# A two-layer macaron transformer block on one Trainium2 core: pairing chunks 1 to 7 of the gated FFN in place of 0 to 5

## The chip, the cores and the metric

The kernel runs on one core of a Trainium2 chip, with no second core to wait for. The metric is device time in microseconds (us): the median of a few executions of the compiled program. Five engines matter here. PE (TensorE) multiplies matrices and accumulates in PSUM banks. DVE (VectorE) and ACT (ScalarE) prepare its operands and empty its banks. SP only issues the DMA transfers that bring weights from HBM, one after the other in a fixed order. POOL (GpSimd) has a few small operations. Each engine works through its own list in order and waits at semaphores for the others.

## The reference

The input is 256 tokens of width 1024, in fp32. Two layers each compute FFN 1, a token mixing of three mixers with one projection in and one out, and FFN 2, each with a residual and a LayerNorm. The part that the change touches is the gated FFN, with an inner width of 2816:

```python
def swiglu(x, w_gate, w_up, w_down):
    return (jax.nn.silu(x @ w_gate) * (x @ w_up)) @ w_down
...
x = layer_norm(ALPHA * x + 0.5 * swiglu(x, ffn1_gate[l], ffn1_up[l], ffn1_down[l]), ln1_g[l], ln1_b[l])
```

There are four such FFNs, named here by layer and place: (0,1), (0,2), (1,1) and (1,2). Between (0,1) and (0,2), and between (1,1) and (1,2), stands the mixing of that layer.

## The kernel before

**Arithmetic.** PE works on fp32 values that are split in two: `hi` is a rounded copy (ACT), `lo` the rest (DVE, `raw - hi`). Every product is three matmuls, hi·hi, hi·lo and lo·hi (`mm3`, L248 to L250, and `proj_chan`, L258 to L260). Weights stream from HBM in blocks of 128 x 1024 fp32 (512 KB) into five `raw` buffers, and from there by one cast and one subtraction (L190, L191) into twelve `hi` and twelve `lo` buffers. `ensure` issues the loads in the order of `_plan`, seven blocks ahead of the one that is being used. A `raw` buffer is free when its last reader is through.

**An FFN.** The inner width is cut into chunk 0 of 512 columns and chunks 1 to 9 of 256. For each chunk PE makes the gate product `pg`, ACT takes its Silu (`sg`, L421), PE makes the up product `pu`, and DVE multiplies the two (`h`, L426). Chunk 0 is made with tokens on the partitions (`tok`, twice 128 tokens), so its `h` has to be transposed by PE (`trans`, L439). Chunks 1 to 9 come out transposed (`chan`, 48 matmuls for each of `pg` and `pu`). `h` is then split into `hTh` and `hTl`, which are the stationary operands of the down projection.

**Pairs.** In three of the four FFNs (all but (0,1)) some chunks don't go through the down projection's eight block products but through seven, M1 to M7, by the Strassen-Winograd scheme. For that a pair of down blocks `ra`, `rb` is combined in `pair_operands`: `b11` and the cast of `rb` (operands 1, 2, 3), four subtractions in place in the `raw` buffers (L202), and then `rest`, which casts the sums `th`, `sh` (operands 5, 7 from `ra`, 4, 6 from `rb`). `rest` waits in the list `put_off` until some further blocks have been cast. The left operands need sums of `h` too (`left_sums`, L461 to L464). A chunk of 256 is one unit of seven products (21 matmuls with 512 columns); chunk 0 is two.

Before the change chunks 0 to 5 are paired. In iteration c (1 to 6) the order on PE is: `pg` of chunk c; M1, M2, M4, M5 of chunk c-1; `pu` of chunk c; M6, M7, M3 of chunk c-1. In these iterations `pg` and `pu` share one PSUM bank (`free`), since the other one (`held`) keeps M3. So `pu` can't start before `sg` has been read out of the bank, nor the next `pg` before `h` has. The four products in the middle stand between `pg` and `pu`, the three at the end between `pu` and the next `pg`. After iteration 6 `combine` adds M1 to M7 into the residual; chunks 6 to 9 go through plain products at the end (`down`).

**What sets the order.** The program is written as straight Python, and a scheduler turns it into a fixed list for each engine, by its own estimates of when data arrive. `high_priority` moves `sg` and `h` forward. Small loads hang behind a given transfer (`issue_after`): the LayerNorm's `lng` and `lnb` in iteration 2, seven small tensors of the mixing in iteration 4 of FFN 1.

Of the kernel before, what the change touches and what calls it, by code (L numbers as in the profile page):

```python
# [17 lines left out]
S = 256  # L18
# [15 lines left out]

def _paired(l, f):

    return 0 if (l, f) == (0, 1) else 6
# [26 lines left out]
def _plan():  # L64

    out = []
    for l in range(L):
        for f in (1, 2):
# [13 lines left out]
            for c, (f0, fw) in enumerate(CHUNKS):  # L82
                for name in ("g", "u"):
                    step = _step(l, f, name, c)
                    out += [((l, f, name, c), k, step * fw, True) for k in range(0, KC, step)]
                out += [((l, f, "d", c), k, 1024, True) for k in range(fw // 128)]
# [46 lines left out]
def _build(tc, A, out):  # L133
# [3 lines left out]
    with ExitStack() as es:  # L137
        pool = lambda name, bufs, **k: es.enter_context(tc.tile_pool(name=name, bufs=bufs, **k))
        cst = pool("cst", 1)
        rawp = pool("raw", 5)  # L140
        hip = pool("hi", 12)
        lop = pool("lo", 12)
# [24 lines left out]
        def ensure(i):  # L167
            while len(loaded) <= min(i, len(plan) - 1):
                key, k, n, split, o = plan[len(loaded)]
                src = A["ws"][o:o + 128 * n].rearrange("(p c) -> p c", p=128)  # L170
                if len(key) == 4 and key[2] == "d" and key[3] < _paired(*key[:2]):
# [21 lines left out]
                while put_off and put_off[0][0] < len(loaded) - 1:  # L193
                    put_off.pop(0)[1]()
# [195 lines left out]
        def ffn(l, f, lni, last=False, mid=None):  # L390
# [17 lines left out]
            def chan(name, c):  # L408

                w = kslices((l, f, name, c), 256)  # L410
                if c <= paired_chunks:
# [19 lines left out]
            def hpair():  # L431
                return (wk.tile([128, 512], F32R, name="hTh", tag="a"),
                        wk.tile([128, 512], F32R, name="hTl", tag="a"))

            def trans(h, t):
# [5 lines left out]
                if paired_chunks:  # L441
                    hf[t] = wk.tile([128, 4, 128], F32, name="hf", tag="w")
                    ACT.copy(hf[t].rearrange("p a b -> p (a b)"), tr)
                    tr = hf[t].rearrange("p a b -> p (a b)")
# [9 lines left out]
            hf = {}  # L454
# [3 lines left out]
            def left_sums(c, i, a11, a12, a21, a22):  # L458

                S = wk.tile([128, 4, 128], F32, name="S", tag="w")  # L460
                DVE.tensor_tensor(S[:, 0, :], a21, a22, ALU.add)  # L461
                DVE.tensor_tensor(S[:, 1, :], S[:, 0, :], a11, ALU.subtract)
                DVE.tensor_tensor(S[:, 2, :], a11, a21, ALU.subtract)
                DVE.tensor_tensor(S[:, 3, :], a12, S[:, 1, :], ALU.subtract)  # L464
# [3 lines left out]
                left[c, i] = {5: part(0), 6: part(1), 7: part(2), 3: part(3)}  # L468

            def left_side(c, i, m):  # L470
                if m in (3, 5, 6, 7):
                    return left[c, i][m]
                t, b = {1: (0, 0), 2: (0, 1), 4: (1, 1)}[m]
                return stationary(c, t, 2 * i + b)

            def paired(c, ms):

                for m in ms:
# [3 lines left out]
                    for i in range(CHUNKS[c][1] // 256):  # L482
                        w = blocks((l, f, "d", c))[2 * i]
                        mm3(M[m], left_side(c, i, m), w[m], c == 0 and i == 0,
                            c == paired_chunks - 1 and i == CHUNKS[c][1] // 256 - 1)
# [46 lines left out]
            else:  # L532
                for t in range(2):
# [3 lines left out]
                    h[t] = product(tok("u", t), sg)  # L537

            if paired_chunks:
                turns.append(1)  # L540
                free, held = f"gu{len(turns) % 2}", f"gu{1 - len(turns) % 2}"
            for c in range(1, n):
# [5 lines left out]
                if c <= paired_chunks:  # L548
                    if c == 1:
                        for i in range(2):  # L550
                            a = lambda t, b: hf[t][:, 2 * i + b, :]
                            left_sums(0, i, a(0, 0), a(0, 1), a(1, 0), a(1, 1))
                    paired(c - 1, (1, 2, 4, 5))
# [8 lines left out]
                if c <= paired_chunks:  # L562
                    paired(c - 1, (6, 7, 3))
                hT[c] = hpair()
                split_to(*hT[c], hc)
                if c < paired_chunks:
# [372 lines left out]
```

## Time and profile before

| what | value |
|---|---|
| runs | 998.08, 990.7, 993.01 us, median 993.01 |
| profiled execution | 994.34 us, its span 992.6 us |
| granted TensorE clock | 0.999 of full speed |
| PE busy | 969.1 us (98%), 6765 instructions |
| DVE busy | 734.8 us (74%) |
| ACT busy | 512.3 us (52%) |
| DMA | 183.19 MB, the weights' queue 55.0% of the 16 engines' span |
| FFN (0,2) | 312.12 to 498.46 us |
| FFN (1,1) | 498.46 to 685.25 us |
| FFN (1,2) | 799.32 to 984.65 us |

Times in the trace count from the span's start. A row of the timeline gives start, duration, engine, line, operation, output and inputs; in square brackets stands how long the engine had been idle before it, and what it waited for. Durations of neighbours overlap by some 0.05 to 0.17 us (an instruction's start, not its end, frees the place for the next), so a step is read from start to start.

### The profile page before, as it was taken

Reading aid. Unit: us, or ns where it says so; the run is one execution under the profiler, and the core shown is the slowest. Engines: PE = TensorE matmul, PEld = TensorE weight load, DVE = VectorE, ACT = ScalarE, POOL = GpSimd, SP = SyncE. Lnnn points to the kernel's source line nnn. Section 1 sums busy time; section 2 is a strip of 40 time slices with the busy share of each in tenths; the row PEclk is TensorE's granted clock in tenths of the full one; section 3 lists DMA queues with packets and bytes.
Section 4 is the critical chain, followed back from the end, with each engine's and each line's share of the span. In section 5 each row is a group of like instructions: output and inputs, shape, how many; then the busy total and the mean of one; then the engine's idle time right before and its main releaser. Section 6 shows DMA issues by size and latency. Waiting matters only on the chain.

```text
span 992.6 us, 16879 instructions
## 1 busy us (share of the span) xinstructions
PE 969.1 (98%) x6765; PEld 875.8 (88%) x6765; DVE 734.8 (74%) x1094; ACT 512.3 (52%) x730; POOL 19.8 (2%) x42
## 2 busy tenths in 40 slices
PE   7999999999999999999999999999999999999996
PEld 5899999899878799999879899998988778989995
DVE  5755454586869978877598888848678797888844
ACT  6644444256556655555255556534475555556520
POOL 1000000010000000000000000000000000000000
PEclk9999999999999999999999999999999999999999
DMA  7977566284323557677245667764742245757611
GB/s 256 344 237 226 181 194 193 96 324 147 111 86 128 179 180 236 194 253 233 86 151 171 233 214 253 237 200 148 256 149 80 84 158 170 253 196 232 213 60 43
DMA packets 53069, 183.19 MB, mean 185 GB/s; under 512 B 6656, under 2 KB 7168, under 8 KB 52992
## 3 DMA queue, kind: packets, MB, share of 16 engines
q1 hardware_dynamic: 52992, 182.12, 55.0%
q8 instruction: 53, 0.87, 0.4%
q14 instruction: 24, 0.20, 0.1%
HBM read 181.05 MB, written 1.05 MB: 183 GB/s over the span
## 4 chain that ended last, share of the span: by engine, by line
PE 74%; DVE 11%; DMA 9%; issue 3%; ACT 3%; SPq 0%; DVEq 0%; ACTq 0%
DMA raw<-in_ws 8%; PE pu L258 6%; PE pu L260 6%; PE pu L259 6%; PE pg L258 5%; PE pg L260 5%; PE pg L259 5%; PE y L248 4%; PE y L250 4%; PE y L249 4%; DVE raw L202 3%; PE pc L258 3%; PE pc L260 3%; PE pc L259 3%; DVE lo L263 3%
## 5 line engine op out<-in xcount | busy, mean ns | idle before, releaser
L191 DVE TENSOR_TENSOR lo<-raw,hi 128x1024 fp32r<-128x1024 f32 (+3 forms) x284 | 336.6, 1200 | 115.2 <-ACT hi L190 113.5
L190 ACT CAST hi<-raw 128x1024 fp32r<-128x1024 f32 (+3 forms) x284 | 289.8, 1034 | 247.4 <-PE pu L259 64.7
L258 PE MATMUL pu<-xTh,hi 128*128 128x256 f32 x576 | 161.7, 281 | 3.4 <-ACT sg L421 3.4
L258 PE MATMUL pg<-xTh,hi 128*128 128x256 f32 x576 | 161.6, 281 | 0.5 <-DVE h L426 0.5
L260 PE MATMUL pu<-xTh,lo 128*128 128x256 f32 x576 | 160.9, 279 | 0.0
L260 PE MATMUL pg<-xTh,lo 128*128 128x256 f32 x576 | 160.8, 279 | 0.0
L259 PE MATMUL pu<-xTl,hi 128*128 128x256 f32 x576 | 160.8, 279 | 0.0
L259 PE MATMUL pg<-xTl,hi 128*128 128x256 f32 x576 | 160.8, 279 | 0.0
L258 PEld LDWEIGHTS pu<-xTh,hi 128*128 128x128 f32 x576 | 108.0, 188 | 7.1 <-ACT sg L421 5.9
L263 ACT CAST hi<-raw 128x1024 fp32r<-128x1024 f32 x63 | 66.2, 1052 | 90.5 <-DVE raw L202 46.5
L258 PEld LDWEIGHTS pg<-xTh,hi 128*128 128x128 f32 x576 | 108.1, 188 | 2.3 <-DVE h L426 1.2
L259 PEld LDWEIGHTS pu<-xTl,hi 128*128 128x128 f32 x576 | 107.9, 187 | 1.2
L260 PEld LDWEIGHTS pu<-xTh,lo 128*128 128x128 f32 x576 | 108.2, 188 | 0.2
L259 PEld LDWEIGHTS pg<-xTl,hi 128*128 128x128 f32 x576 | 107.9, 187 | 0.5
L260 PEld LDWEIGHTS pg<-xTh,lo 128*128 128x128 f32 x576 | 108.2, 188 | 0.0
L263 DVE TENSOR_TENSOR lo<-raw,hi 128x1024 fp32r<-128x1024 f32 x63 | 76.7, 1219 | 30.6 <-ACT hi L263 21.7
L258 PE MATMUL pc<-xTh,hi 128*128 128x256 f32 x256 | 73.0, 285 | 0.5 <-DVE kd L630 0.5
L248 PE MATMUL y<-hi,hTh 128*128 128x512 f32 x184 | 72.4, 394 | 0.0
L260 PE MATMUL pc<-xTh,lo 128*128 128x256 f32 x256 | 72.4, 283 | 0.0
L259 PE MATMUL pc<-xTl,hi 128*128 128x256 f32 x256 | 71.8, 281 | 0.0
L250 PE MATMUL y<-hi,hTl 128*128 128x512 f32 x184 | 71.8, 390 | 0.0
L249 PE MATMUL y<-lo,hTh 128*128 128x512 f32 x184 | 71.6, 389 | 0.0
(188 smaller groups left out, 1702.0 us busy)
## 6 DMA issues: line engine op xcount, KB each, us to landing
raw<-in_ws SPq DMA_DIRECT2D x312, 512.0 KB, 4.6
w<-in_ws SPq DMA_DIRECT2D x8, 512.0 KB, 6.2
lng<-in_ln SPq DMA_DIRECT2D x6, 512.0 KB, 6.8
lnb<-in_ln SPq DMA_DIRECT2D x6, 512.0 KB, 7.7
raw<-in_ws SPq DMA_DIRECT2D x8, 256.0 KB, 4.8
raw<-in_ws SPq DMA_DIRECT2D x4, 420.0 KB, 4.3
x<-in_x SPq DMA_DIRECT2D x4, 256.0 KB, 5.6
out<-x SPq DMA_DIRECT2D x4, 256.0 KB, 2.1
```

The lines of the kernel that those rows point to most:

```text
L190: splits.append((ACT.copy(hi, raw), DVE.tensor_tensor(lo, raw, hi.bitcast(F32), ALU.subtract)))
L191: DVE.tensor_tensor(lo, raw, hi.bitcast(F32), ALU.subtract)))
L202: sub = lambda o, i, j: DVE.tensor_tensor(o, i, j, ALU.subtract)
L248: PE.matmul(o, lhsT=a[0], rhs=b[0], start=start, stop=False)
L249: PE.matmul(o, lhsT=a[0], rhs=b[1], start=False, stop=False)
L250: return PE.matmul(o, lhsT=a[1], rhs=b[0], start=False, stop=stop)
L258: PE.matmul(p[:, b, :], lhsT=hi, rhs=xTh[:, k, :], start=k == 0, stop=False)
L259: PE.matmul(p[:, b, :], lhsT=hi, rhs=xTl[:, k, :], start=False, stop=False)
L260: PE.matmul(p[:, b, :], lhsT=lo, rhs=xTh[:, k, :], start=False, stop=k == KC - 1)
L263: return ACT.copy(hi, src), DVE.tensor_tensor(lo, src, hi.bitcast(F32), ALU.subtract)
```

## The change

`_paired` gives 7, and the pairs are chunks 1 to 7; they are worked in iterations 2 to 8. Chunk 0 takes no part: its four down blocks move in the load order from behind `u` of chunk 0 to between `u` and `d` of chunk 9, and are used plainly in the last products, in the order 8, 0, then 9. So the number of units (7) and of matmuls stays. The copy of the transposed `h` of chunk 0 (`hf`, two on ACT for each of three FFNs) is gone, and `left_sums` has one caller. The put-off casts wait for one more block (`- 2` in place of `- 1`), and M3 and M4 change places: M1, M2, M3, M5 stand behind `pg`, and M6, M7, M4 behind `pu`. Twelve buffers in place of nine serve the tag `a`. Buffer counts of `raw`, `hi` and `lo` stay (5, 12, 12); left out below are the lines that only name them, and three in the mixing that repeat the count of tag `a`. Lines of the changed kernel stand 5 lines further down around the casts (L191 is L196, L202 L207, L263 L268, L421 L426, L426 L431).

```diff
--- before.py
+++ after.py
@@
 
 
 
+RAW, SPLIT = 5, 12
+
+
 def _paired(l, f):
 
-    return 0 if (l, f) == (0, 1) else 6
+    return 0 if (l, f) == (0, 1) else 7
 
 
 def _w_in_groups():
@@
                 for name in ("g", "u"):
                     step = _step(l, f, name, c)
                     out += [((l, f, name, c), k, step * fw, True) for k in range(0, KC, step)]
-                out += [((l, f, "d", c), k, 1024, True) for k in range(fw // 128)]
+
+                for c in ([0, c] if c == len(CHUNKS) - 1 else [c] if c else []) if _paired(l, f) else [c]:
+                    out += [((l, f, "d", c), k, 1024, True) for k in range(CHUNKS[c][1] // 128)]
     return out
 
 
@@
             while len(loaded) <= min(i, len(plan) - 1):
                 key, k, n, split, o = plan[len(loaded)]
                 src = A["ws"][o:o + 128 * n].rearrange("(p c) -> p c", p=128)
-                if len(key) == 4 and key[2] == "d" and key[3] < _paired(*key[:2]):
+                if len(key) == 4 and key[2] == "d" and 0 < key[3] <= _paired(*key[:2]):
                     raw = rawp.tile([128, n], F32, name="raw", tag="raw")
                     stream.append(SP.dma_start(raw, src))
                     if k % 2 == 0:
@@
                 splits.append((ACT.copy(hi, raw),
                                DVE.tensor_tensor(lo, raw, hi.bitcast(F32), ALU.subtract)))
                 loaded.append((hi, lo))
-                while put_off and put_off[0][0] < len(loaded) - 1:
+                while put_off and put_off[0][0] < len(loaded) - 2:
                     put_off.pop(0)[1]()
 
         def pair_operands(ra, rb):
@@
             def chan(name, c):
 
                 w = kslices((l, f, name, c), 256)
-                if c <= paired_chunks:
+                if 1 < c <= paired_chunks + 1:
                     p = ps.tile([128, 2, 256], F32, name="p" + name, tag=free, bufs=1)
                 else:
                     p = gu_bank([128, 2, 256], "p" + name)
@@
             hT = {}
 
             def hpair():
-                return (wk.tile([128, 512], F32R, name="hTh", tag="a"),
-                        wk.tile([128, 512], F32R, name="hTl", tag="a"))
+                return (wk.tile([128, 512], F32R, name="hTh", tag="a", bufs=12),
+                        wk.tile([128, 512], F32R, name="hTl", tag="a", bufs=12))
 
             def trans(h, t):
                 tr = ps.tile([128, 512], F32, name="tr", tag="tr")
@@
                     c = slice(i * 128, i * 128 + 128)
                     PE.transpose(tr[:, c], h[:, c], ident)
                 hT[0, t] = hpair()
-                if paired_chunks:
-                    hf[t] = wk.tile([128, 4, 128], F32, name="hf", tag="w")
-                    ACT.copy(hf[t].rearrange("p a b -> p (a b)"), tr)
-                    tr = hf[t].rearrange("p a b -> p (a b)")
                 split_to(*hT[0, t], tr)
 
             def stationary(c, t, i):
@@
                 s = slice(i * 256 + t * 128, i * 256 + t * 128 + 128)
                 return hT[c][0][:, s], hT[c][1][:, s]
 
-            hf = {}
             left = {}
             M = {}
 
-            def left_sums(c, i, a11, a12, a21, a22):
-
+            def left_sums(c, h):
+
+                A = {(t, b): h[:, b * 256 + t * 128:b * 256 + t * 128 + 128] for t in range(2) for b in range(2)}
                 S = wk.tile([128, 4, 128], F32, name="S", tag="w")
-                DVE.tensor_tensor(S[:, 0, :], a21, a22, ALU.add)
-                DVE.tensor_tensor(S[:, 1, :], S[:, 0, :], a11, ALU.subtract)
-                DVE.tensor_tensor(S[:, 2, :], a11, a21, ALU.subtract)
-                DVE.tensor_tensor(S[:, 3, :], a12, S[:, 1, :], ALU.subtract)
+                DVE.tensor_tensor(S[:, 0, :], A[1, 0], A[1, 1], ALU.add)
+                DVE.tensor_tensor(S[:, 1, :], S[:, 0, :], A[0, 0], ALU.subtract)
+                DVE.tensor_tensor(S[:, 2, :], A[0, 0], A[1, 0], ALU.subtract)
+                DVE.tensor_tensor(S[:, 3, :], A[0, 1], S[:, 1, :], ALU.subtract)
                 hi, lo = hpair()
                 split_to(hi, lo, S.rearrange("p a b -> p (a b)"))
                 part = lambda j: (hi[:, j * 128:j * 128 + 128], lo[:, j * 128:j * 128 + 128])
-                left[c, i] = {5: part(0), 6: part(1), 7: part(2), 3: part(3)}
-
-            def left_side(c, i, m):
-                if m in (3, 5, 6, 7):
-                    return left[c, i][m]
-                t, b = {1: (0, 0), 2: (0, 1), 4: (1, 1)}[m]
-                return stationary(c, t, 2 * i + b)
+                left[c] = {5: part(0), 6: part(1), 7: part(2), 3: part(3),
+                           1: stationary(c, 0, 0), 2: stationary(c, 0, 1), 4: stationary(c, 1, 1)}
 
             def paired(c, ms):
 
+                w = blocks((l, f, "d", c))[0]
                 for m in ms:
                     if m not in M:
                         tag, bufs = {3: (held, 1), 6: ("tr", 2), 7: ("tr", 2)}.get(m, ("y", 4))
                         M[m] = ps.tile([128, 512], F32, name=f"M{m}", tag=tag, bufs=bufs)
-                    for i in range(CHUNKS[c][1] // 256):
-                        w = blocks((l, f, "d", c))[2 * i]
-                        mm3(M[m], left_side(c, i, m), w[m], c == 0 and i == 0,
-                            c == paired_chunks - 1 and i == CHUNKS[c][1] // 256 - 1)
+                    mm3(M[m], left[c][m], w[m], c == 1, c == paired_chunks)
 
             def combine():
 
@@
                     if t == 1:
                         trans(h[0], 0)
                     h[t] = product(tok("u", t), sg)
-
-            if paired_chunks:
-                turns.append(1)
-                free, held = f"gu{len(turns) % 2}", f"gu{1 - len(turns) % 2}"
             for c in range(1, n):
+                in_pairs = 1 < c <= paired_chunks + 1
+                if in_pairs and c == 2:
+
+                    turns.append(1)
+                    free, held = f"gu{len(turns) % 2}", f"gu{1 - len(turns) % 2}"
                 p = chan("g", c)
                 with tc.high_priority(offset=60):
                     sg = gated(p)
                 if c == 1:
                     trans(h[1], 1)
-                if c <= paired_chunks:
-                    if c == 1:
-                        for i in range(2):
-                            a = lambda t, b: hf[t][:, 2 * i + b, :]
-                            left_sums(0, i, a(0, 0), a(0, 1), a(1, 0), a(1, 1))
-                    paired(c - 1, (1, 2, 4, 5))
+                if in_pairs:
+                    paired(c - 1, (1, 2, 3, 5))
                 elif not paired_chunks:
                     if c > 1 and c - 2 < n - late:
                         down([c - 2], 1)
@@
                 pu = chan("u", c)
                 with tc.high_priority(offset=60):
                     hc = product(pu, sg)
-                if c <= paired_chunks:
-                    paired(c - 1, (6, 7, 3))
+                if in_pairs:
+                    paired(c - 1, (6, 7, 4))
                 hT[c] = hpair()
                 split_to(*hT[c], hc)
-                if c < paired_chunks:
-                    a = lambda t, b: hc[:, b * 256 + t * 128:b * 256 + t * 128 + 128]
-                    left_sums(c, 0, a(0, 0), a(0, 1), a(1, 0), a(1, 1))
-                if c == paired_chunks:
+                if c <= paired_chunks:
+                    left_sums(c, hc)
+                if paired_chunks and c == paired_chunks + 1:
                     combine()
                 if c == 2:
                     with tc.issue_after(stream[-1].ins):
@@
                     with tc.issue_after(stream[-1].ins):
                         mid()
 
-            down(range(n - late, n - 1), 0)
+            cs = [*range(paired_chunks + 1, n - 1), 0] if paired_chunks else [*range(n - late, n - 1)]
+            down(cs, 0)
             down([n - 1], 0, end=True)
-            done = down(range(n - late, n), 1, end=True)
+            done = down([*cs, n - 1], 1, end=True)
             coef = 1.0 if paired_chunks else 2 * ALPHA
             layer_norm(0, y[0], coef, 4 * EPS, gb, last, [done[9], done[14]])
             layer_norm(1, y[1], coef, 4 * EPS, gb, last)
```

How the instructions move is shown at three places. Numbers behind names only tell tiles apart.

**DVE at the head of FFN (0,2)**, from the split of the last transposed input `xTl` to the first `h` of chunk 0 (`h_3546` before, `h_3527` now). Before:

```order
L263 TENSOR_TENSOR xTl_89<-tr_3411,xTh_88 128x4x128
L202 TENSOR_TENSOR raw_3432<-raw_3432,raw_3430 128x512
L263 TENSOR_TENSOR lo_3480<-raw_3474,hi_3479 128x1024
L202 TENSOR_TENSOR raw_3432<-raw_3432 128x512
L202 TENSOR_TENSOR raw_3445<-raw_3445 128x512
L191 TENSOR_TENSOR lo_3490<-raw_3487,hi_3489 128x1024
L202 TENSOR_TENSOR raw_3445<-raw_3474,raw_3445 128x512
L263 TENSOR_TENSOR lo_3494<-raw_3430,hi_3493 128x1024
L202 TENSOR_TENSOR raw_3474<-raw_3474,raw_3445 128x512
L263 TENSOR_TENSOR lo_3498<-raw_3432,hi_3497 128x1024
L202 TENSOR_TENSOR raw_3474<-raw_3474 128x512
L426 TENSOR_TENSOR h_3546<-pu_3521,sg_3472 128x512
```

Now:

```order
L196 TENSOR_TENSOR lo_3445<-raw_3442,hi_3444 128x1024
L268 TENSOR_TENSOR xTl_89<-tr_3402,xTh_88 128x4x128
L268 TENSOR_TENSOR xTl_89<-tr_3411,xTh_88 128x4x128
L196 TENSOR_TENSOR lo_3478<-raw_3475,hi_3477 128x1024
L431 TENSOR_TENSOR h_3527<-pu_3502,sg_3473 128x512
L268 TENSOR_TENSOR b11_3485<-raw_3481,b11_3485 128x512
```

Before, ten instructions on down weights of chunk 0 and other blocks stand between `xTl` and `h`; now one does, and the pair's `b11` follows behind `h`.

**ACT ahead of `sg` in a middle iteration of FFN (0,2)**: from the `sg` of one chunk to that of the next. Before:

```order
L421 ACTIVATE sg_4136<-pg_4087 128x512
L263 CAST hi_4077<-raw_4048 128x1024
L190 CAST hi_4083<-raw_4081 128x1024
L190 CAST hi_4152<-raw_4150 128x1024
L263 CAST b11_4233<-raw_4156 128x512
L263 CAST hi_4236<-raw_4231 128x1024
L190 CAST hi_4246<-raw_4244 128x1024
L263 CAST hTh_4218<-h_4207 128x512
L190 CAST hi_4252<-raw_4250 128x1024
L263 CAST hTh_4227<-S_4222 128x512
L263 CAST hi_4256<-raw_4156 128x1024
L421 ACTIVATE sg_4319<-pg_4270 128x512
```

Now:

```order
L426 ACTIVATE sg_4209<-pg_4160 128x512
L195 CAST hi_4225<-raw_4223 128x1024
L268 CAST b11_4306<-raw_4229 128x512
L268 CAST hi_4309<-raw_4304 128x1024
L195 CAST hi_4319<-raw_4317 128x1024
L195 CAST hi_4325<-raw_4323 128x1024
L268 CAST hTh_4291<-h_4280 128x512
L195 CAST hi_4331<-raw_4329 128x1024
L268 CAST hTh_4300<-S_4295 128x512
L268 CAST hi_4335<-raw_4229 128x1024
L268 CAST hi_4339<-raw_4304 128x1024
L426 ACTIVATE sg_4392<-pg_4343 128x512
```

Here `b11_4233`, `hi_4236` (of `rb`) and `hi_4256` (of `th`) belong to one pair, and so do `b11_4306`, `hi_4309`, `hi_4335` and `hi_4339` (of `sh`). Before, `b11` stands four rows behind the first `sg`, and `th` right ahead of the second, with `sh` behind it; now `b11` stands two rows behind, and `th` and `sh` both ahead of the second `sg`.

**DVE in the same iteration**, from the sums of `h` to the `lo` of `th` (`lo_4257` before, `lo_4336` now). Before:

```order
L463 TENSOR_TENSOR S_4222<-h_4207 128x128
L263 TENSOR_TENSOR hTl_4219<-h_4207,hTh_4218 128x512
L462 TENSOR_TENSOR S_4222<-S_4222,h_4207 128x128
L202 TENSOR_TENSOR raw_4156<-raw_4156 128x512
L464 TENSOR_TENSOR S_4222<-h_4207,S_4222 128x128
L202 TENSOR_TENSOR raw_4156<-raw_4231,raw_4156 128x512
L191 TENSOR_TENSOR lo_4247<-raw_4244,hi_4246 128x1024
L263 TENSOR_TENSOR hTl_4228<-S_4222,hTh_4227 128x512
L202 TENSOR_TENSOR raw_4231<-raw_4231,raw_4156 128x512
L191 TENSOR_TENSOR lo_4253<-raw_4250,hi_4252 128x1024
L202 TENSOR_TENSOR raw_4231<-raw_4231 128x512
L263 TENSOR_TENSOR lo_4257<-raw_4156,hi_4256 128x1024
```

Now:

```order
L207 TENSOR_TENSOR raw_4304<-raw_4304,raw_4229 128x512
L462 TENSOR_TENSOR S_4295<-h_4280 128x128
L464 TENSOR_TENSOR S_4295<-h_4280 128x128
L463 TENSOR_TENSOR S_4295<-S_4295,h_4280 128x128
L207 TENSOR_TENSOR raw_4304<-raw_4304 128x512
L268 TENSOR_TENSOR hTl_4292<-h_4280,hTh_4291 128x512
L465 TENSOR_TENSOR S_4295<-h_4280,S_4295 128x128
L196 TENSOR_TENSOR lo_4320<-raw_4317,hi_4319 128x1024
L268 TENSOR_TENSOR hTl_4301<-S_4295,hTh_4300 128x512
L196 TENSOR_TENSOR lo_4326<-raw_4323,hi_4325 128x1024
L196 TENSOR_TENSOR lo_4332<-raw_4329,hi_4331 128x1024
L268 TENSOR_TENSOR lo_4336<-raw_4229,hi_4335 128x1024
```

Before, all four subtractions of the pair (`raw_4156`, `raw_4231`) stand between `h_4207` and the `lo` of `th`; now the two on `raw_4229` stand ahead of `h_4280`, two are left behind it, and three plain `lo` stand there in place of two.

## Rows read from the trace of the kernel before

**Rows 1.** Page, part 1: busy time, share of the span, instructions.

```profile
PE 969.1 (98%) x6765; PEld 875.8 (88%) x6765; DVE 734.8 (74%) x1094; ACT 512.3 (52%) x730; POOL 19.8 (2%) x42
```

**Rows 2.** Waits of PE: total us, times, longest; waits elsewhere left out.

```profile
PE tr L439 <- DVE h L426: 4.5, 3, 1.8
PE pu L258 <- ACT sg L421: 3.4, 6, 1.2
...
PE pg L258 <- DVE h L426: 0.5, 1, 0.5
```

**Rows 3.** Timeline, PE, head of FFN (0,2): start, us, operation, [idle before].

```profile
331.74 0.63 PE L439 MATMUL tr<-ident,h 128*128 128x128 f32 x4 [1.77 <-DVE h L426]
```

**Rows 4.** Timeline, DVE, the same head: `xTl`, the last L202, `h`.

```profile
321.56 1.28 DVE L263 TENSOR_TENSOR xTl<-tr,xTh 128x512 fp32r<-128x512 f32 x2
...
330.31 0.68 DVE L202 TENSOR_TENSOR raw<-raw 128x512 f32<-128x512 f32 x1
330.91 0.68 DVE L426 TENSOR_TENSOR h<-pu,sg 128x512 f32<-128x512 f32 x1
```

**Rows 5.** Timeline, PE, one iteration of FFN (0,2) without a wait: `pg` to `pg`.

```profile
392.55 0.28 PE L258 MATMUL pg<-xTh,hi 128*128 128x256 f32 x1
...
408.69 0.28 PE L258 MATMUL pg<-xTh,hi 128*128 128x256 f32 x1
```

**Rows 6.** Timeline, PE, FFN (1,1): M1 behind `pg`, the waiting `pu`, M6.

```profile
567.62 0.39 PE L248 MATMUL M<-b,hTh 128*128 128x512 f32 x1
...
571.71 0.39 PE L258 MATMUL pu<-xTh,hi 128*128 128x256 f32 x1 [1.18 <-ACT sg L421]
...
577.47 0.40 PE L248 MATMUL M<-hi,hTh 128*128 128x512 f32 x1
```

**Rows 7.** Timeline, ACT, the cast of `th` and `sg`, iteration 5 of FFN (0,2).

```profile
414.81 1.06 ACT L263 CAST hi<-raw 128x1024 fp32r<-128x1024 f32 x1 [2.38 <-DVE raw L202]
415.77 0.59 ACT L421 ACTIVATE sg<-pg 128x512 f32<-128x512 f32 x1
```

**Rows 8.** Timeline, PE, iteration 1 of FFN (0,2), products mixed with `pu`.

```profile
343.82 0.47 PE L248 MATMUL M<-b,hTh 128*128 128x512 f32 x1
...
355.38 0.39 PE L248 MATMUL M<-hi,hTh 128*128 128x512 f32 x1
```

**Rows 9.** Timeline, PE, FFN (0,1): `pg` behind `pu`, then the first down product.

```profile
88.22 0.28 PE L258 MATMUL pg<-xTh,hi 128*128 128x256 f32 x1
...
93.88 0.40 PE L248 MATMUL y<-hi,hTh 128*128 128x512 f32 x1
```

**Rows 10.** Timeline, DVE, the same chunks of FFN (0,1).

```profile
88.01 1.23 DVE L191 TENSOR_TENSOR lo<-raw,hi 128x1024 fp32r<-128x1024 f32 x1 [5.66 <-ACT hi L190]
89.16 0.68 DVE L426 TENSOR_TENSOR h<-pu,sg 128x512 f32<-128x512 f32 x1
```

**Rows 11.** Timeline, ACT, the same chunks of FFN (0,1): a cast, then `sg`.

```profile
94.00 1.05 ACT L190 CAST hi<-raw 128x1024 fp32r<-128x1024 f32 x1 [0.37 <-PE pg L259]
94.96 0.59 ACT L421 ACTIVATE sg<-pg 128x512 f32<-128x512 f32 x1
```

**Rows 12.** Timeline, DVE, sums of `h` in FFN (0,2).

```profile
408.95 0.28 DVE L463 TENSOR_TENSOR S<-h 128x128 f32<-128x128 f32 x1
409.15 0.28 DVE L462 TENSOR_TENSOR S<-S,h 128x128 f32<-128x128 f32 x1
```

**Rows 13.** Page, part 6, DMA issues: count, KB each, median us to landing.

```profile
raw<-in_ws SPq DMA_DIRECT2D x312, 512.0 KB, 4.6
...
lnb<-in_ln SPq DMA_DIRECT2D x6, 512.0 KB, 7.7
```

**Rows 14.** Timeline, SP's queue, FFN (1,1): `ra`, seven small loads (left out), `rb`.

```profile
586.94 0.33 SPq L173 DMA_DIRECT2D raw<-in_ws  x1
...
591.06 0.33 SPq L173 DMA_DIRECT2D raw<-in_ws  x1
```

**Rows 15.** Timeline, ACT: the cast of that `rb`.

```profile
596.90 1.05 ACT L263 CAST hi<-raw 128x1024 fp32r<-128x1024 f32 x1 [0.71 <-DMA raw<-in_ws]
```

More of the change, by code (lines that the diff above doesn't have):

```diff
@@ L139, in _build @@
         cst = pool("cst", 1)
-        rawp = pool("raw", 5)
-        hip = pool("hi", 12)
-        lop = pool("lo", 12)
+        rawp = pool("raw", RAW)
+        hip = pool("hi", SPLIT)
+        lop = pool("lo", SPLIT)
         wk = pool("wk", 9)
@@ L624, in mixing @@
             for i in range(2):
-                kd = wk.tile([128, 2, 16, 16], F32, name="kd", tag="a")
+                kd = wk.tile([128, 2, 16, 16], F32, name="kd", tag="a", bufs=12)
                 pe = sp["pe"][:, i, None, :]
@@ L822, in attend @@
                 DVE.tensor_reduce(nm[:, :m], sc, AX.X, ALU.max, negate=True)
-                P = wk.tile([128, m, w], F32, name="P", tag="a")
+                P = wk.tile([128, m, w], F32, name="P", tag="a", bufs=12)
                 su = sm.tile([128, 4], F32, name="su")
@@ L837, in attend @@
                     PE.transpose(tr[:, i, :], Pv[:, i * 128:i * 128 + 128], ident)
-                PT = wk.tile([128, 4, 128], F32, name="PT", tag="a")
+                PT = wk.tile([128, 4, 128], F32, name="PT", tag="a", bufs=12)
                 ACT.copy(PT, tr)
```

## The prediction

> **What bounds the kernel now.** I read the page's busy times first. PE is busy 98% of the span, DVE 74%, ACT 52% [rows 1]. So PE's list of matmuls sets the time, and since the change leaves their number as it is, only the stretches in which PE stands still or stumbles can be won. The waits of PE name them: three transpositions wait for `h`, 4.5 us together, six `pu` wait for `sg`, 3.4 us, and one `pg` waits for `h`, 0.5 us [rows 2]. That is 8.4 us in ten waits, all in the three FFNs with pairs. The timeline then tells what stands behind each of them.
>
> At the head of an FFN DVE goes from `xTl` at 321.56 to `h` at 330.91, and what lies between is work on down blocks, the last of it a subtraction of a pair, at 330.31 [rows 4]; PE's transposition had waited 1.77 us when it began at 331.74 [rows 3]. In a middle iteration the cast of `th` stands ahead of `sg` on ACT and waits 2.38 us for a subtraction on DVE, so `sg` comes late however early `pg` was [rows 7].
>
> The iteration without a wait is the measure: from one `pg` to the next 16.14 us [rows 5]. A `pg` of 48 matmuls takes 5.66 us (93.88 - 88.22) [rows 9], so 21 products of 512 columns take 16.14 - 2 x 5.66 = 4.82 us, 0.23 us (0.2295) each. Hence the cover that the shared bank leaves: four products between `pg` and `pu`, 12 matmuls, 2.75 us for `sg`; three between `pu` and the next `pg`, 2.07 us for `h`.
>
> **What the change takes away.**
>
> *Idle time*: 8.4 us [rows 2], if no wait comes back.
>
> *Restarts*: a wait costs more than its idle time. From M1 at 567.62 to the waiting `pu` at 571.71 are 4.09 us; 2.75 of products and 1.18 of idle time leave 0.16. That `pu` then takes 5.76 us (to 577.47) in place of 5.66, 0.10 more [rows 6]. Ten waits at 0.26: 2.6 us.
>
> *Mixed products*: in iteration 1 the 24 matmuls of chunk 0 are mixed with `pu`; from 343.82 to 355.38 are 11.56 us [rows 8], where 24 x 0.2295 + 5.66 = 11.17 would do. The 24 go to the last products, which PE does in one run: 0.39 x 3 = 1.2 us. The sum of all three is 12.2 us.
>
> *Cost nothing either way*: six copies `hf` are gone from ACT, which is idle half of the time; four casts and four `lo` of chunk 0's blocks replace its pair work, at the end of the FFN in place of the head. There the last iteration has no pair left to prepare, so its DVE time covers them; without that cover each `lo` would cost its 1.15 us (89.16 - 88.01) [rows 10]. Buffers of tag `a` cost no time. `combine` falls two iterations later; `pg`, `pu` of chunk 9, 11.3 us, stand behind it, ahead of the last products.
>
> **Whether the waits really go.** At the head: the transposition would have started at 331.74 - 1.77 = 329.97, and `pg` of the second half, 24 x 0.2295 = 5.5 us, stands ahead of it, so the `pu` that `h` needs ended at about 324.4. DVE has `xTl` done at 322.8 and one `lo` of 1.15 left, until 324.0. `h` can follow its `pu` directly, some 4 us before it is needed. These three waits go.
>
> In the iterations I take the pace from FFN (0,1), which has the order now given to the others: a `lo` whose buffer a late matmul of `pu` frees, then `h`. There `h` starts at 89.16, 0.94 after `pu`'s end (88.22), and ends 1.62 after it [rows 9, 10]. From `h`'s end to the matmul that waited for it passes 0.15 us (330.91 + 0.68 to 331.74) [rows 3, 4]. So 1.77 of the cover of 2.07 are used, 0.3 us are spare. `sg` has the cast of `sh` ahead of it, which a late matmul of `pg` frees; in FFN (0,1) the same stands there, and `sg` starts at 94.96 and ends 1.67 after `pg`'s end at 93.88 [rows 9, 11]. With 0.15 that is 1.82 of 2.75; 0.9 us are spare. `th` no longer waits for a subtraction right ahead of it: its two stand ahead of `h` now.
>
> M5 is the product that the later `rest` could make wait. Counted from `pu`'s end by DVE's list: `h` at 0.94, then 0.60 for each step of 128 x 512 [rows 4] and 0.20 for each sum [rows 12]: `h`, a subtraction, three sums, a subtraction, `hTl`, a sum come to 4.14; `lo` 1.15 to 5.29, `hTl` to 5.89, two more `lo` to 8.19, the `lo` of `th` to 9.34. M5's second matmul, the first that reads it, comes at 2.07 + 5.66 + 10 x 0.2295 = 10.02. With 0.15, 0.5 us are spare.
>
> The five `raw` buffers are the last condition. `rb` can be issued when the third plain `lo` is through, at 8.19. The chain behind it is its cast (1.05, the length in [rows 15]), `lo` 1.15 and `h` 0.68, and `h` must end by 16.14 + 2.07 - 0.15 = 18.06, so a landing time of up to 7.0 us costs nothing. The median is 4.6 [rows 13]. Two places are tighter. In FFN (1,1) seven small loads stand between `ra` and `rb`: 4.12 us in the queue (586.94 to 591.06) [rows 14], and `rb`'s cast began 5.84 after that issue [rows 15]. `ra` goes out at 7.04, so `rb` is there at 17.0. A subtraction that reads it (0.60) and `h` (0.68) end at 18.3, 0.24 late: 0.5 with a restart; were cast and `lo` ahead of `h`, 2.1. In iteration 2 of each FFN `lng` and `lnb` go ahead of `rb`, two issues or 0.9 us; with 4.6 to land nothing is late, with 7.7 as `lnb` itself [rows 13] it is 1.6 + 0.26, 5.6 for three. I take 0.3 each, 0.9, since most loads land in 4.6. What stays is 0.5 + 0.9 = 1.4, between 0.5 and 7.7.
>
> One row and one rule disagree. By the rows, each hand-over of the shared bank is covered, 1.82 of 2.75 and 1.77 of 2.07 us. The Trainium skill (Perfetto Trace Analysis, Optimizing Tensor Performance, Matmuls) has independent groups of matmuls rotate through different PSUM banks, so that the evacuation of one overlaps the next; here seven iterations, not six, go through one bank. By the rows that costs nothing, by the rule it is a rival below.
>
> **Sum.** 12.2 - 1.4 = 10.8 us. The profiled execution of 994.34 (span 992.6) becomes 983.5; the median, 993.01, lies 1.3 below the profiled one and becomes **982.2**.
>
> **Rivals.**
>
> *Only the head is won* (0.24). Head waits and mixed products go, 4.5 + 3 x 0.26 + 1.2 = 6.5 us, but `h` and `sg` are late as often as before: 3.9 + 7 x 0.26 = 5.7 us stay, and a sixth comes on top, since seven iterations share a bank. 5.5 us are won: 987.5. For it speaks the spare of only 0.3 us, against it FFN (0,1), which shows no such wait.
>
> *The raw ring starves* (0.09; slower). `rest` reads `ra` and `rb` later, so two of five buffers come free later, and each `rb` lands late. It decides from a landing of 7.0 us on; at `lnb`'s 7.7 each of 21 iterations loses 0.7 + 0.26, 20 us, and the kernel comes to 993.0 - 12.2 + 20.2 = 1001. Against it speaks the median of 4.6.
>
> *The bank is not handed over in time* (0.05). If the added iteration of each FFN pays both evacuations in full, 1.82 + 1.77 = 3.6 us, three of them take 10.8 of the 12.2: 991.6. This is what the skill's rule on rotating banks would come to; the rows show the cover that speaks against it.
>
> *The change doesn't move what waits* (0.02), about 993. The list of DVE shows ten instructions ahead of `h` cut to one, so hardly.
>
> **Chances and range.** The forecast has 0.60. About 1% is what a measurement of this kernel can tell from no change, so faster means below 983.1. That takes a residue of up to 2.3 us in place of 1.4; about five sixths of the forecast's weight, 0.50, with 0.02 of the first rival. Within 1%: 0.39. Slower: 0.09. The range runs from 979.5 (the full 12.2 and 1.3 of scatter) to 992.0, which takes in the first and the third rival; above it lies the starved ring, and with it some 0.15 in all are left out.
>
> **What would show it.** Right: no wait of a transposition for `h`; at most a few tenths of `pu` for `sg`; an iteration of 16.14 us nearly everywhere; `sg` ending about 1.7 and `h` about 1.6 us after their products; stages (0,2) and (1,2) some 3 to 4 us shorter, and (1,1) too, less its one wait at the small loads. Wrong: a `pg` or M5 that waits in most iterations (the spares of 0.3 and 0.5 were not there), casts of `rb` that wait for DMA with `h` behind them (the ring), or `lo` of chunk 0's blocks that hold up the last products.

## The result, and the profile after

The changed kernel takes 982.32 us (median of 4 runs, 981.7 to 983.14) beside 992.95 for the kernel before: a ratio of 0.9886, 95% interval 0.9847 to 0.9925. The forecast was 982.2. The profiled execution took 983.14 us, its span is 981.3, at a granted clock of 0.997.

Part 1 of the page of the changed kernel, which answers to [rows 1]:

```profile
PE 966.0 (98%) x6761; PEld 876.2 (89%) x6765; DVE 737.5 (75%) x1094; ACT 512.4 (52%) x724; POOL 19.0 (2%) x42
```

The matmuls are the same in number (four records are missing from this trace); PE is busy 3.1 us less. DVE is busy 2.7 us longer, and ACT, with its six copies less, as long as before. Of the 11.3 us by which the two spans differ, the other 8.2 are idle time of PE. The waits of PE in the changed kernel (total us, times, longest), as the view lists them, beside [rows 2]:

```profile
PE tr L285 <- POOL blk L335: 3.5, 1, 3.5
PE tr L285 <- DMA x<-in_x: 1.4, 1, 1.4
PE pg L263 <- DVE h L431: 1.0, 1, 1.0
PE pg L253 <- ACT hi L195: 0.9, 1, 0.9
```

The first, second and fourth belong to the start of the program, which the change doesn't touch. Of the ten waits of 8.4 us one of 1.0 is left. The lengths of the stages, from the first `pg` of an FFN to the first matmul of what follows (to the start of the last product for (1,2)), tell where the time went, in us. The table has the experiments too, told below.

| kernel | FFN (0,2) | FFN (1,1) | FFN (1,2) | median of its runs |
|---|---|---|---|---|
| before | 186.34 | 186.79 | 185.10 | 992.95 to 993.99 |
| the change | 182.52 | 183.78 | 181.36 | 982.32 |
| the change, run again | 182.53 | 183.02 | 181.36 | 982.36 |
| pairs_only | 183.46 | 184.22 | 182.01 | 984.09 |
| old_products | 182.65 | 182.66 | 181.62 | 981.69 |
| early_casts | 182.52 | 183.33 | 181.35 | 981.63 |
| put_off_only | 187.15 | 186.91 | 185.27 | 995.87 |
| before_loads_late | 184.86 | 185.50 | 183.21 | 989.51 |
| put_off_loads_late | 185.06 | 184.44 | 183.83 | 987.36 |
| mid_late | 182.52 | 182.53 | 181.35 | 980.99 |
| three_front | 182.57 | 183.46 | 181.35 | 981.29 |
| raw4 | 191.50 | 189.59 | 186.86 | 1007.25 |
| raw6 | 182.52 | 183.04 | 181.35 | 982.96 |

The three FFNs give 10.57 of the 11.2 us by which the two profiled executions differ. The rest lies in the program's start, before any pair: up to the first mixing it takes 198.0 us before and 197.1 now, and 196.1 to 197.7 in the profiled executions of the experiments.

**The head.** Timelines of PE and of DVE in the changed kernel, beside [rows 3, 4]:

```profile
328.66 0.40 PE L255 MATMUL pg<-hi,xTl 128*128 128x512 f32 x1
328.90 0.60 PE L444 MATMUL tr<-ident,h 128*128 128x128 f32 x4
```

```profile
320.17 1.37 DVE L268 TENSOR_TENSOR xTl<-tr,xTh 128x512 fp32r<-128x512 f32 x2
321.45 1.22 DVE L196 TENSOR_TENSOR lo<-raw,hi 128x1024 fp32r<-128x1024 f32 x1
323.49 0.69 DVE L431 TENSOR_TENSOR h<-pu,sg 128x512 f32<-128x512 f32 x1 [0.83 <-PE pu L255]
```

DVE now waits for `pu`, 0.83 us, with nothing of the pairs in between: `h` ends at 324.18, 4.7 us before the transposition begins, without a wait.

**An iteration.** DVE and ACT of the changed kernel in one iteration of FFN (0,2), whose `pu` ended at 393.03 and whose next `pg` ended at 400.76:

```profile
392.82 1.23 DVE L268 TENSOR_TENSOR lo<-raw,hi 128x1024 fp32r<-128x1024 f32 x1 [1.38 <-ACT hi L268]
393.96 0.68 DVE L431 TENSOR_TENSOR h<-pu,sg 128x512 f32<-128x512 f32 x1
...
401.19 2.35 DVE L268 TENSOR_TENSOR lo<-raw,hi 128x1024 fp32r<-128x1024 f32 x2
```

```profile
401.18 1.05 ACT L268 CAST hi<-raw 128x1024 fp32r<-128x1024 f32 x1 [0.64 <-PE pg L265]
402.13 0.59 ACT L426 ACTIVATE sg<-pg 128x512 f32<-128x512 f32 x1
```

`h` starts 0.93 after `pu`'s end and ends 1.61 after it; so it does, within 0.03, in 17 of the 21 iterations; in two it is earlier, and in two, at the small loads and right behind them, later. The `lo` of `th` starts at 8.16 (forecast 8.19). `sg` ends 1.96 after `pg` here and 1.67 to 1.69 after it in the 20 others (forecast 1.67).

**The wait that is left.** FFN (1,1), iteration 4: SP's queue, DVE and PE, beside [rows 14, 15]:

```profile
566.58 0.33 SPq L178 DMA_DIRECT2D raw<-in_ws  x1
...
571.08 0.33 SPq L178 DMA_DIRECT2D raw<-in_ws  x1
```

```profile
577.44 0.69 DVE L207 TENSOR_TENSOR raw<-raw 128x512 f32<-128x512 f32 x1 [4.29 <-DMA raw<-in_ws]
578.04 0.68 DVE L431 TENSOR_TENSOR h<-pu,sg 128x512 f32<-128x512 f32 x1
```

```profile
578.78 0.38 PE L263 MATMUL pg<-xTh,hi 128*128 128x256 f32 x1 [0.98 <-DVE h L431]
```

`rb` is issued 4.5 us behind `ra`, after the seven small loads, and lands some 6.3 us later (forecast 4.12 and 5.84). The subtraction that reads it stands ahead of `h`, and `h` ends 3.16 after `pu`, past the cover of 2.07.

### The profile page after: what moved, and what is told of

The parts are those of the page before. It is cut to its first block, busy times and chain, and to the rows that moved or that the text cites. A ratio compares the mean times of both kernels' runs of the same rounds, so it can differ in the third digit from the quotient of the medians.

```text
span 981.3 us, 16914 instructions
## 1 busy us (share of the span) xinstructions
PE 966.0 (98%) x6761; PEld 876.2 (89%) x6765; DVE 737.5 (75%) x1094; ACT 512.4 (52%) x724; POOL 19.0 (2%) x42
## 4 chain that ended last, share of the span: by engine, by line
PE 95%; DMA 2%; DVE 1%; issue 0%; ACT 0%; SPq 0%; DVEq 0%; ACTq 0%
PE pg L263 7%; PE pu L263 7%; PE pg L265 7%; PE pg L264 7%; PE pu L265 7%; PE pu L264 7%; PE y L253 4%; PE y L255 4%; PE y L254 4%; PE M L253 3%; PE M L255 3%; PE pc L263 3%; PE pc L265 3%; PE M L254 3%; PE pc L264 3%; DMA raw<-in_ws 2%
## 5 line engine op out<-in xcount | busy, mean ns | idle before, releaser
L196 DVE TENSOR_TENSOR lo<-raw,hi 128x1024 fp32r<-128x1024 f32 (+3 forms) x284 | 336.8, 1200 | 105.9 <-ACT hi L195 96.7
L263 PE MATMUL pg<-xTh,hi 128*128 128x256 f32 x576 | 161.4, 280 | 1.0 <-DVE h L431 1.0
L263 PE MATMUL pu<-xTh,hi 128*128 128x256 f32 x576 | 161.6, 280 | 0.0
L263 PEld LDWEIGHTS pg<-xTh,hi 128*128 128x128 f32 x576 | 108.1, 188 | 2.3 <-DVE h L431 1.4
L263 PEld LDWEIGHTS pu<-xTh,hi 128*128 128x128 f32 x576 | 108.1, 188 | 1.1
L268 ACT CAST hi<-raw 128x1024 fp32r<-128x1024 f32 x63 | 66.0, 1051 | 77.2 <-PE pu L264 35.1
L268 DVE TENSOR_TENSOR lo<-raw,hi 128x1024 fp32r<-128x1024 f32 x63 | 75.2, 1220 | 19.5 <-ACT hi L268 19.5
L263 PE MATMUL pc<-xTh,hi 128*128 128x256 f32 x256 | 73.2, 286 | 0.1
```

The costliest lines, as they stand in the source:

```text
L196: DVE.tensor_tensor(lo, raw, hi.bitcast(F32), ALU.subtract)))
L263: PE.matmul(p[:, b, :], lhsT=hi, rhs=xTh[:, k, :], start=k == 0, stop=False)
L268: return ACT.copy(hi, src), DVE.tensor_tensor(lo, src, hi.bitcast(F32), ALU.subtract)
```

## The experiments

The first four take the change apart, the next two settle what they left open, and the others test the wait at the small loads, the covers and the ring of `raw` buffers.

**pairs_only**: the chunks alone.

```diff
-                while put_off and put_off[0][0] < len(loaded) - 2:
+                while put_off and put_off[0][0] < len(loaded) - 1:
-                    paired(c - 1, (1, 2, 3, 5))
+                    paired(c - 1, (1, 2, 4, 5))
-                    paired(c - 1, (6, 7, 4))
+                    paired(c - 1, (6, 7, 3))
```

> Pairs 1 to 7 and chunk 0 at the end, but casts put off and products ordered as before (M1, M2, M4, M5 behind pg; M6, M7, M3 behind pu). Theory (the head goes with chunk 0, the waits of the iterations go with the order of the products): no wait of a transposition, but about seven waits of pu for sg or pg for h stay, 4 us idle and 6 us in all, so about 987.5. Rival (moving the pairs away from the head takes all waits along): about 982.3, no wait of pu for sg.

Measured: 984.09 us, ratio 0.9904 (0.9874 to 0.9934). The theory was mostly wrong. Three waits of `pu` stay, one in each FFN:

```profile
PE pu L263 <- ACT sg L426: 2.1, 3, 1.3
```

They stand in the last paired iteration of (0,2) and of (1,2) and at the small loads of (1,1). The waits of iteration 3 are gone without the longer put-off or the new order of products. Of the 11.8 us that the three FFNs lose beyond their best lengths in the table, the chunks alone give 8.5.

**old_products**: the change with the products in their old order.

```diff
-                    paired(c - 1, (1, 2, 3, 5))
+                    paired(c - 1, (1, 2, 4, 5))
-                    paired(c - 1, (6, 7, 4))
+                    paired(c - 1, (6, 7, 3))
```

> The changed kernel with M4 back in front and M3 at the end; casts still put off by one block more. Theory (with M3 last, the buffers of rb come free late, so b11 waits for the 35th matmul of pu and the cast of rb for the 47th; the subtractions come behind h, and th waits for them ahead of sg): waits of pu for sg come back, about 987.5. Rival (it is the longer put-off that takes th away from the subtractions): no wait, 982.3.

Measured: 981.69 us, ratio 0.9886 (0.9858 to 0.9913); in the profile no wait of PE at all behind the start. The theory fell.

**early_casts**: the change with the old put-off.

```diff
-                while put_off and put_off[0][0] < len(loaded) - 2:
+                while put_off and put_off[0][0] < len(loaded) - 1:
```

> The changed kernel with the casts put off as before (one block less), products in the new order. Theory (the order of the products does it; the put-off moves only one cast past another, each of them freed by a late matmul of pg): no wait, 982.3 as the change. Rival (the put-off does it): waits of pu for sg come back, 987.5.

Measured: 981.63 us, ratio 0.9883 (0.985 to 0.9917); one wait in the iterations, 0.5 us of `pg` for `h` at the small loads. Here the theory's number came, and so the rival of this run fell too: with the chunks moved, either the longer put-off or the new order of products was enough for the last 2 us. For the put-off, part of this hangs on a small margin (see Open).

**put_off_only**: the longer put-off and the new order, with pairs 0 to 5.

```diff
-                while put_off and put_off[0][0] < len(loaded) - 1:
+                while put_off and put_off[0][0] < len(loaded) - 2:
-                    paired(c - 1, (1, 2, 4, 5))
+                    paired(c - 1, (1, 2, 3, 5))
-                    paired(c - 1, (6, 7, 3))
+                    paired(c - 1, (6, 7, 4))
```

> The kernel before, pairs 0 to 5, with the longer put-off and the new order of products. Theory: the three transpositions still wait for h, 4.5 us, and the mixed products stay, but no pu waits for sg: 993.0 - 5.7 = 987.3. Rival (the waits of the iterations come from chunk 0's double share of DVE work at the head): no gain, 993.

Measured: 995.87 us, ratio 1.0021 (1.0004 to 1.0039). No gain: in the profiled executions the three FFNs together are 1.1 us longer than before. No `pu` waits for `sg` any more, as the theory had it, but `pg` waits for `h` instead; waits of PE:

```profile
PE pg L258 <- DVE h L426: 5.4, 4, 1.8
PE tr L439 <- DVE h L426: 4.4, 3, 1.6
```

The longest, 1.84 us, is the `pg` of iteration 3 in FFN (0,2). On DVE, shortly ahead of it:

```profile
373.68 0.69 DVE L202 TENSOR_TENSOR raw<-raw 128x512 f32<-128x512 f32 x1 [2.12 <-DMA raw<-in_ws]
374.77 1.23 DVE L263 TENSOR_TENSOR lo<-raw,hi 128x1024 fp32r<-128x1024 f32 x1 [0.40 <-ACT hi L263]
375.91 0.68 DVE L426 TENSOR_TENSOR h<-pu,sg 128x512 f32<-128x512 f32 x1
```

A subtraction waits for `rb`, and `h` stands behind it. So the cause of the iterations' waits lies one step further back than I had looked: `rb` is late. In iteration 2 `ra`, `lng`, `lnb`, `rb` leave SP's queue in this order in the kernel before, the change and these four alike. In the kernel before (SP's queue, then the cast of that `rb` on ACT; `pg` of iteration 2 begins at 359.48, its `pu` ends at 373.55):

```profile
367.36 0.33 SPq L173 DMA_DIRECT2D raw<-in_ws  x1
367.74 0.42 SPq L355 DMA_DIRECT2D lng<-in_ln  x1
...
369.10 0.33 SPq L173 DMA_DIRECT2D raw<-in_ws  x1
```

```profile
376.99 1.05 ACT L263 CAST hi<-raw 128x1024 fp32r<-128x1024 f32 x1 [3.15 <-DMA raw<-in_ws]
```

And in the changed kernel (`pg` of iteration 2 begins at 346.68, its `pu` ends at 360.74):

```profile
347.73 0.33 SPq L178 DMA_DIRECT2D raw<-in_ws  x1
...
349.46 0.33 SPq L178 DMA_DIRECT2D raw<-in_ws  x1
```

```profile
359.45 1.05 ACT L268 CAST hi<-raw 128x1024 fp32r<-128x1024 f32 x1 [3.28 <-PE pu L264]
```

Before, `rb` goes out 9.6 us after `pg`'s start and its cast waits for the transfer until 3.4 us after `pu`'s end. Now it goes out 2.8 us after `pg`'s start, and its cast waits only for a buffer that `pu` frees. The loads are the same; the iteration in which they fall no longer has chunk 0's down blocks in the `raw` ring ahead of it. In FFN (0,2) `rb` goes out 2.8 us after that `pg`'s start in each run with pairs 1 to 7 and five `raw` buffers, whatever the put-off and the order of products.

**before_loads_late**: the kernel before, with these loads behind the last pair.

```diff
-                if c == 2:
+                if c == (8 if paired_chunks else 2):
-                if c == 4 and mid:
+                if c == (9 if paired_chunks else 4) and mid:
```

> The kernel before (pairs 0 to 5), with lng and lnb loaded in iteration 8 in place of 2 and the seven small loads in iteration 9 of FFN (1,1) in place of 4, that is behind the last pair. New theory (the waits of iterations 3 and 5 come from rb queued behind these loads, which the moved pairs meet earlier in their iteration): the four waits of iteration 3 (0.52, 0.48, 1.18, 0.72 us) and that of iteration 5 (0.23) go, with restarts 4.4 us; the three transpositions (4.5 us) and the waits of iteration 6 (0.43, 0.27) stay: 988.7 beside 993.1. Rival (chunk 0's double share of pair work on DVE at the head makes the iterations late): the waits stay, 993.

Measured: 989.51 us, ratio 0.9958 (0.9945 to 0.9972). The new theory holds. No wait of `pu` for `sg` is left in the list, those of iteration 6 are gone too, which I had not expected; the three transpositions still wait 4.2 us, and of the four waits of iteration 3 one stays, `pg` for `h` in (1,1), 0.8 us. The three FFNs are 4.7 us shorter than before (forecast 4.4). The two loads had cost `rb` its landing more than its place in the queue: in iteration 2 of FFN (0,2) it goes out 9.6 us after `pg`'s start with them and 9.4 without, but it takes 7.8 and 4.4 us to land. The issue of that one `rb`, in the kernel before and in this run (KB, us to landing):

```profile
raw<-in_ws SPq DMA_DIRECT2D x1, 512.0 KB, 7.8
```

```profile
raw<-in_ws SPq DMA_DIRECT2D x1, 512.0 KB, 4.4
```

**put_off_loads_late**: put_off_only with the same two lines.

> put_off_only (pairs 0 to 5, longer put-off, new order of products), with the same loads moved behind the last pair. New theory (with the new order of products the subtraction that reads rb stands ahead of h, so the same late rb now stops pg, 5.4 us in four waits): these four go, 6.4 us with restarts, and no pu waits for sg: 995.9 - 6.4 = 989.5, with the transpositions (4.4 us) left. Rival (the new order fits pairs 0 to 5 badly by itself): waits of pg for h stay, 994 to 996.

Measured: 987.36 us, ratio 0.9942 (0.9926 to 0.9958). No `pg` waits for `h`: the same late `rb` had only stopped another matmul. The three FFNs are 6.0 us shorter than in put_off_only (forecast 6.4); the medians differ by 8.5, with runs of put_off_only from 993.57 to 999.23. What is left are the three transpositions, 4.6 us, and 0.9 us of M products that wait for `hTh`, in iteration 1 where they are mixed with `pu`.

**mid_late**: the change, with the small loads in iteration 9 of FFN (1,1).

```diff
-                if c == 4 and mid:
+                if c == (9 if paired_chunks else 4) and mid:
```

> The changed kernel with the seven small loads of the mixing issued in iteration 9 of FFN (1,1) in place of 4, where no pair is loaded. Theory (the one wait left, 0.98 us of pg for h, comes from these loads between ra and rb): the wait is gone, 1.25 us with its restart, and nothing comes in its place: 981.1 beside 982.3. Rival (rb lands late there for another reason, or the loads delay the mixing): the wait stays or a new one stands at the head of the mixing, 982.3 or above.

Measured: 980.99 us, ratio 0.9865 (0.9841 to 0.989). No wait is left behind the start, (1,1) takes 182.53, as long as (0,2), and the mixing behind it 114.01 (114.23 in the change).

**after_again** and **mid_late_again**: the change and mid_late, both unaltered, side by side.

> The changed kernel unaltered, on the same chip as the next one: 982.3, one wait of pg for h of 1.0 us.

> mid_late unaltered, beside the changed kernel: 1.2 us less than it, by the wait that it leaves out and its restart, 981.1.

Measured: 982.36 us, ratio 0.9889 (0.9874 to 0.9904), and 981.07, ratio 0.988 (0.986 to 0.99). In the profile of the first, `rb` came 5.2 us after its issue, not 6.3. The list shows no wait of `pg` there, though `pg` began 0.24 us later than its pace; (1,1) was still 0.4 us longer than in the second. So the size of the wait depends on the execution. The 1.3 us between the two kernels came out alike in both pairs of medians, but the intervals overlap: likely better, not shown beyond doubt.

**three_front**: less cover for `sg`, more for `h`.

```diff
-                    paired(c - 1, (1, 2, 3, 5))
+                    paired(c - 1, (1, 2, 3))
-                    paired(c - 1, (6, 7, 4))
+                    paired(c - 1, (5, 7, 6, 4))
```

> The changed kernel with three products behind pg (M1, M2, M3) and four behind pu (M5, M7, M6, M4), so the cover for sg is 2.07 us and that for h 2.76. Theory (sg ends 1.68 us after pg and 0.15 pass until pu begins, so 0.24 are spare): no wait of pu; the wait of pg in FFN (1,1) shrinks by 0.69 to some 0.3: about 981.6. Rival (a shared bank costs something even where it is covered, or sg is late by more than the trace shows): 21 waits of pu for sg of 0.3 us and more, 988 or above.

Measured: 981.29 us, ratio 0.9868 (0.9847 to 0.9889). The theory holds: no `pu` waits, though in one iteration `sg` ended 1.97 after `pg` and `pu` began at 2.08, its place in the other iterations. There the first matmul of `pu` took 0.05 us longer, and that is all. Only the `pg` at the small loads waits, 0.7 us (forecast 0.3).

**raw4** and **raw6**: four or six `raw` buffers (raw6 with ten of tag `a`).

```diff
-RAW, SPLIT = 5, 12
+RAW, SPLIT = 4, 12
```

> The changed kernel with four raw buffers in place of five. Theory (the ring of raw buffers has some 1.5 us to spare per iteration, since rb is issued 8.2 us behind pu's end and may take 7.0 to land; with four it is issued two casts later): rb lands about 1 us too late in each of the 21 iterations, with restarts some 27 us: about 1010, casts waiting for DMA. Rival (loads land early enough that the ring doesn't matter): 982 to 985.

> The changed kernel with six raw buffers (and ten in place of twelve of tag a, to make room). Theory (the ring costs nothing except in the iteration with the small loads, where an earlier ra moves rb forward by one cast, 1.15 us): the wait of 0.98 us goes, 981.1. Rival (loads are late in other places too, hidden in what is counted as restarts): 979 or below.

Measured: 1007.25 us, ratio 1.0143 (1.0099 to 1.0188), and 982.96, ratio 0.9885 (0.9864 to 0.9907). Waits with four buffers:

```profile
ACT hi L195 <- DMA raw<-in_ws: 127.4, 117, 4.5
...
ACT hi L268 <- DMA raw<-in_ws: 35.8, 18, 4.9
...
PE pg L263 <- DVE h L431: 13.9, 15, 2.0
```

With five the first two are 28.3 and 5.7 us. Four buffers turn the transfers' landing into waits of `pg`, as the sum over `rb` had it (1010), though in 15 places and not in 21. In the profiled executions the three FFNs are 20 us longer than in the change, and the second mixing 4. A sixth buffer gains nothing: the wait at the small loads shrinks to 0.25 us, but the median doesn't fall, so the theory's 981.1 was too low.

## Why the prediction was right, and where its reasons were not

**The sum.** 12.2 us could go by the forecast, 1.4 stay. Against the best lengths in the table (182.52, 182.53, 181.35) the three FFNs lost 11.8 before and 1.25 after, all of that in (1,1). Waits, restarts and mixed products were sized rightly.

**The head** was right in place and size. `before_loads_late` and `put_off_loads_late` keep its three waits, 4.2 and 4.6 us in all, whatever else is done, and every kernel with pairs 1 to 7 is free of them.

**The iterations: the right amount from the wrong cause.** The step that failed is the reading of [rows 7]: "so `sg` comes late however early `pg` was", put down to the order of casts and subtractions and cured by the later `rest`. Those rows stem from an iteration in which PE lost nothing: `sg` ended 2.0 us after `pg`, inside the cover of 2.75, and `pu` began without idle time:

```profile
417.10 0.28 PE L258 MATMUL pu<-xTh,hi 128*128 128x256 f32 x1
```

In pairs_only the cast of `th` waits as long for a subtraction in eight iterations, and `sg` ends 1.60 to 1.65 after `pg` in each of them; one, of FFN (0,2):

```profile
368.39 1.05 ACT L268 CAST hi<-raw 128x1024 fp32r<-128x1024 f32 x1 [2.38 <-DVE raw L207]
```

So a subtraction ahead of that cast costs nothing by itself. Where `pu` did wait, in iterations 3 and 5, the last releaser was a subtraction too, but the reading stopped at it. It had come late because `rb` had, and `rb` because other loads were issued right ahead of it, `lng` and `lnb` for the waits of iteration 3, the seven small ones for that of iteration 5, while the `raw` ring was already behind. (In iteration 6 the cast ahead of `sg` is a plain one and waits for its own block.) The longer put-off and the new order alone, without the chunks, make the kernel no faster (ratio 1.0021, 1.0004 to 1.0039); with the chunks they give some 2 us. `before_loads_late` takes the listed waits for `sg` away with two lines of load order. What ties this to the chunks: with chunk 0's down blocks moved the same loads leave 2.8 in place of 9.6 us after `pg`'s start. That the waits went as forecast was therefore luck as far as this step goes: the change held a cure that the prediction hadn't seen.

**`lng` and `lnb`** were given 0.9 us of residue; they cost nothing now, by the same rows. **The small loads** were given 0.5, and cost 1.25 in one profiled execution and 0.5 in another, there without a listed wait. Two errors and a right sum: 1.4 forecast, 1.25 found; this, too, is luck.

**M5** was argued wrongly. The `lo` of `th` does start at 8.16 after `pu`'s end, as worked out, but PE's list has the M5 that reads it behind the `pg` after the next, an iteration of 16.14 us later. The spare is 16.6 us, not 0.5. No result hung on it.

**The rivals.** Only the head is won: no. The starved ring: not at five buffers, but at four. In the changed kernel `rb` went out 8.3 us behind `pu`'s end (8.19 forecast), which is why that rival could be priced. The bank: each `sg` and `h` ended inside the cover, but for the `h` at the small loads, and three_front, with 0.7 us less cover for `sg`, was no slower. The Trainium skill (Perfetto Trace Analysis, Optimizing Tensor Performance, Matmuls) has groups rotate through the banks so that the evacuation of one overlaps the matmuls of the next. Here other products lay between, and the overlap was there on one bank.

**Open.** In the last paired iteration of (0,2) and (1,2) a plain cast stands ahead of `sg` and waits for its block. With the old order of products (before, before_loads_late, pairs_only, old_products) that block leaves 2.4 us after `pg`'s start in all four. In before and pairs_only it took 4.8 to 5.1 us to land, and `pu` waited 0.26 to 0.54; in the two others it took 4.2 to 4.4, and `sg` ended 2.57 to 2.75 after `pg`, at the edge of the cover. The cast in (0,2), in pairs_only and in old_products:

```profile
450.92 1.05 ACT L195 CAST hi<-raw 128x1024 fp32r<-128x1024 f32 x1 [1.79 <-DMA raw<-in_ws]
```

```profile
450.35 1.06 ACT L195 CAST hi<-raw 128x1024 fp32r<-128x1024 f32 x1 [1.14 <-DMA raw<-in_ws]
```

So half a microsecond of landing time decides these waits. Whether the longer put-off, or the moved loads, make the block land sooner or the executions happened to differ is not shown. With the new order (early_casts, the change) that cast waits only for `pg`, and `sg` ends at 1.67. That chunk 0's down blocks are what had delayed `ra` and `rb` in iteration 2 is read from the queues; moving them alone was not tried.

## What to carry to other kernels

When an engine waits for a cast that waits for a subtraction, follow the chain until it reaches a transfer or work that was never late; the last releaser is only the last. Before moving arithmetic, look at what else is queued between two transfers that are needed together: two lines that moved the loads of the LayerNorm and of the mixing gave, on the kernel before, 4.7 of the 10.6 us that the whole change gave in these stages. A wait that ends inside its cover costs nothing, so read the chain in an iteration in which the bottleneck waits. And where two edits both cure a wait, take them apart on the chip, since one of them may be what lets a late transfer reach the bottleneck.

## What the runs showed of the hardware

A 512 KB transfer of the same place in the program landed 6.3 us after its issue in one execution and 5.2 in another, with the small loads ahead of it both times; the median of all is 4.7. `rb` of iteration 2, issued right behind `lng` and `lnb` (512 KB each), took 6.5 to 8.6 us to land in the eleven runs that have them in this place (four or five `raw` buffers), and 4.4 to 4.7 in the two without. Between the end of the read that empties a bank and the matmul that writes it next 0.11 us were enough without a wait (three_front).
